# A hybrid decoder layer on one core: the weight products of both half-steps by a block method with seven products

## The chip, the cores and the metric

The kernel runs on one core of one Trainium2 chip. The metric is the device time of that core in microseconds, from launch to end, as the median of several executions. A core has five engines, each with a queue that it works off in order: TensorE (PE, with its weight loads listed as PEld), VectorE (DVE), ScalarE (ACT), GpSimd (POOL) and SyncE (SP), which here only issues DMA transfers. TensorE writes its products to PSUM, which has eight banks of 128 partitions x 512 float32.

## What is computed

512 tokens with 1024 features pass through three parts: a SwiGLU half-step, a mixer (retention heads beside block-sparse attention heads) and a second SwiGLU half-step. All of it is float32. The half-step, with a hidden width of 2816:

```python
def _swiglu(h, w_gate, w_up, w_down):
    return (jax.nn.silu(h @ w_gate) * (h @ w_up)) @ w_down
x = x + 0.5 * _swiglu(_rms(x, ffn1_norm_w[l]), ffn1_w_gate[l], ffn1_w_up[l], ffn1_w_down[l])
```

## The kernel before

Activations lie with their features on the partitions and the 512 tokens along the free axis. Every float32 operand of a product is split exactly into two float32r parts, a high part (a copy on ScalarE, rounded) and a low part (the difference, on VectorE). A product of two such operands is then three matmuls, high x high, high x low and low x high (`mm3`, line 357). Each matmul takes a weight block of 128 x 128 as its stationary operand and all 512 tokens as its moving one.

`ffn` (line 413) is a half-step. For each of 22 blocks of the hidden features it loads the gate and the up weights as chunks of 128 x 1024 (`split_w`, line 329: one DMA of 512 KB on SyncE's queue, one ScalarE copy, one VectorE subtraction) and issues 2 x 8 x 3 = 48 matmuls into two PSUM banks. VectorE and ScalarE then scale by the norm, apply SiLU and multiply, and the result is split into its two parts. For each of 8 blocks of the output features it then loads three chunks of the down weights and issues 22 x 3 = 66 matmuls; VectorE adds half of the sum to the residual, and the next stage's weighted parts are made (`Stream.add`). The last block of the second half-step is done by halves of the tokens, 132 matmuls of 256 columns. The first half-step has 22 x 48 + 8 x 66 = 1584 matmuls, the second 66 more.

The matmuls are started with the unscaled input: the norm's factor per token (`st.r`) is applied behind the products, so that the statistics of the tokens (`Stream.stats`) run beside the first of them.

Nothing is issued in program order. `Plan` (line 63) records every instruction with what it reads and writes, and `_order` (line 193) then runs a list schedule: each engine is modelled with a cost per instruction (`_cost`, line 118), the instruction that was noted first goes first unless the table `DELAYS` shifts its part of the mixer, and an instruction is held back while its tile has no free slot. The instructions are issued in that order, which fixes the order on each engine; on the chip, semaphores make each wait for what it needs. Because `issue` calls all of them from one place, the profile lists them all under line 181.

On-chip memory is 80 tiles of 128 x 512 float32 and three buffers each of 128 x 1024 for a raw weight chunk and its two parts. PSUM has fixed tags: two banks "p", two "s", three "t", one "o".

GpSimd has little to do: sums of squares for the norms and part of the rotations in the mixer. In the body of a half-step it is idle.

## Time and profile before

| | |
|---|---|
| median of 3 runs | 1011.9 us (1011.61 to 1012.08) |
| span of the profiled execution | 1010.4 us, 11674 instructions |
| median less that span | 1.5 us |
| PE busy | 993.1 us (98%), 4524 matmuls |
| DVE busy | 526.2 us (52%) |
| ACT busy | 413.3 us (41%) |
| POOL busy | 88.8 us (9%) |
| granted TensorE clock | 0.998 of full speed |
| DMA | 105.17 MB, mean 104 GB/s |

The span is the time from the first to the last instruction of one profiled execution; the runs' times hold a little more around it. Busy time counts an instruction from its start to its end as the profiler has it. Matmuls are pipelined, so that the busy time of PE and the length of one matmul say little; the distance from one start to the next, or a stretch's length over the matmuls in it, says what one costs. An instruction that is held up by another engine's use of a shared resource is listed as longer, not as waiting.

### The profile page before, as it was taken

Reading aid. Unit: us, or ns where it says so; the run is one execution under the profiler, and the core shown is the slowest. Engines: PE = TensorE matmul, PEld = TensorE weight load, DVE = VectorE, ACT = ScalarE, POOL = GpSimd, SP = SyncE. Lnnn points to the kernel's source line nnn. Section 1 sums busy time; section 2 is a strip of 40 time slices with the busy share of each in tenths; the row PEclk is TensorE's granted clock in tenths of the full one; section 3 lists DMA queues with packets and bytes.
Section 4 is the critical chain, followed back from the end, with each engine's and each line's share of the span. In section 5 each row is a group of like instructions: output and inputs, shape, how many; then the busy total and the mean of one; then the engine's idle time right before and its main releaser. Section 6 shows DMA issues by size and latency. Waiting matters only on the chain.

```text
span 1010.4 us, 11674 instructions
## 1 busy us (share of the span) xinstructions
PE 993.1 (98%) x4524; PEld 812.5 (80%) x4524; DVE 526.2 (52%) x768; ACT 413.3 (41%) x641; POOL 88.8 (9%) x63
## 2 busy tenths in 40 slices
PE   8999999999999999989999999999999999999998
PEld 4888888888888888878887778688888888888888
DVE  7535434534332325587879997855445445432231
ACT  6423223223222225467868876543233233221120
POOL 4000000000010100143213320400000000000000
PEclk9999999999999999999999999999999999999999
DMA  6322322332333463352233211422322322333330
GB/s 222 117 92 84 114 95 84 106 103 78 111 116 105 131 211 115 107 151 66 83 131 115 58 38 53 141 103 86 105 94 94 104 91 97 99 94 110 125 111 26
DMA packets 36407, 105.17 MB, mean 104 GB/s; under 512 B 4480, under 2 KB 6528, under 8 KB 36352
## 3 DMA queue, kind: packets, MB, share of 16 engines
q1 hardware_dynamic: 36352, 104.43, 32.1%
q8 instruction: 35, 0.57, 0.2%
q14 instruction: 20, 0.16, 0.0%
HBM read 97.60 MB, written 4.19 MB: 101 GB/s over the span
## 4 chain that ended last, share of the span: by engine, by line
PE 87%; DVE 7%; ACT 3%; issue 1%; DMA 1%; SPq 0%; DVEq 0%; ACTq 0%
PE ps_p L181 45%; PE ps_s L181 36%; DVE s L181 5%; PE ps_t L181 4%; ACT s L181 2%; PE ps_o L181 2%; DVE wl L181 1%; ACT wh L181 1%; DMA s<-in_x_t_dram 1%; SPq L181 0%; DVE c L181 0%; DVE ad L181 0%; ACT c L181 0%; DVEq L181 0%; ACT cr L181 0%
## 5 line engine op out<-in xcount | busy, mean ns | idle before, releaser
L181 PE MATMUL ps_p<-s,wh 128*128 128x512 f32 (+1 forms) x1548 | 561.8, 392 | 3.1 <-DVE s L181 1.6
L181 PE MATMUL ps_s<-s,wh 128*128 128x512 f32 (+1 forms) x1056 | 399.1, 385 | 0.0
L181 ACT ACTIVATE wh<-raw 128x1024 fp32r<-128x1024 f32 (+4 forms) x186 | 181.0, 976 | 469.7 <-PE ps_p L181 335.7
L181 PEld LDWEIGHTS ps_p<-s,wh 128*128 128x128 f32 x1548 | 289.6, 189 | 67.0 <-DVE s L181 3.4
L181 PE MATMUL ps_p<-s,wl 128*128 128x512 f32 (+1 forms) x774 | 298.3, 392 | 1.7 <-DVE wl L181 1.7
L181 DVE TENSOR_TENSOR wl<-raw,wh 128x1024 fp32r<-128x1024 f32 (+4 forms) x186 | 219.3, 1182 | 131.4 <-ACT wh L181 128.7
L181 PEld LDWEIGHTS ps_s<-s,wh 128*128 128x128 f32 x1056 | 198.6, 188 | 39.5 <-ACT wh L181 0.2
L181 PE MATMUL ps_s<-s,wl 128*128 128x512 f32 (+1 forms) x528 | 203.6, 386 | 1.5 <-DVE wl L181 1.5
L181 PEld LDWEIGHTS ps_p<-s,wl 128*128 128x128 f32 x774 | 145.7, 189 | 32.2 <-DVE wl L181 2.9
L181 ACT ACTIVATE s<-s 128x512 f32<-128x512 f32 (+2 forms) x216 | 134.1, 628 | 77.5 <-DVE s L181 66.8
L181 DVE TENSOR_TENSOR s<-ps_p,s 128x512 f32<-128x512 f32 x72 | 49.5, 688 | 190.8 <-PE ps_p L181 190.0
L181 POOL TENSOR_TENSOR s<-s 128x512 f32<-128x512 f32 x57 | 87.5, 1542 | 376.5 <-ACT s L181 290.6
L181 DVE TENSOR_TENSOR s<-s 128x512 fp32r<-128x512 f32 (+2 forms) x155 | 111.8, 723 | 15.7 <-ACT s L181 8.6
L181 PEld LDWEIGHTS ps_s<-s,wl 128*128 128x128 f32 x528 | 99.1, 188 | 22.7 <-DVE wl L181 3.2
L181 DVE TENSOR_TENSOR s<-ps_s,s 128x512 f32<-128x512 f32 x44 | 30.4, 691 | 52.5 <-PE ps_s L181 50.2
L181 PE MATMUL ps_o<-s 128*128 128x256 f32 (+3 forms) x144 | 39.7, 295 | 2.3 <-DVE s L181 2.1
L181 PE MATMUL ps_t<-wh,s 128*128 128x512 f32 x96 | 33.7, 395 | 0.0
L181 PEld LDWEIGHTS ps_o<-s 128*128 128x128 f32 x144 | 27.3, 189 | 6.8 <-ACT s L181 2.5
L181 DVE SCALAR_TENSOR_TENSOR s<-s 128x512 f32<-128x512 f32 x30 | 24.1, 807 | 11.8 <-ACT s L181 11.5
L181 DVE SCALAR_TENSOR_TENSOR s<-s,cols 128x512 fp32r<-128x512 f32 (+1 forms) x28 | 26.8, 967 | 5.8 <-ACT s L181 5.8
L181 DVE SCALAR_TENSOR_TENSOR s<-ps_p,s 128x512 f32<-128x512 f32 (+1 forms) x9 | 6.0, 662 | 31.1 <-PE ps_p L181 31.1
L181 PE MATMUL ps_s<-s 128*128 128x128 f32 (+3 forms) x64 | 19.0, 336 | 2.8 <-DVE s L181 2.8
(65 smaller groups left out, 387.3 us busy)
## 6 DMA issues: line engine op xcount, KB each, us to landing
raw<-in_wg_dram SPq DMA_DIRECT2D x43, 512.0 KB
raw<-in_wu_dram SPq DMA_DIRECT2D x43, 512.0 KB
raw<-in_wd_dram SPq DMA_DIRECT2D x32, 512.0 KB
raw<-in_w_int_dram SPq DMA_DIRECT2D x20, 512.0 KB
raw<-in_wd_dram SPq DMA_DIRECT2D x16, 384.0 KB
s<-in_rtab_dram SPq DMA_DIRECT2D x16, 256.0 KB
raw<-in_w_inn_dram SPq DMA_DIRECT2D x8, 512.0 KB
raw<-in_w_o_dram SPq DMA_DIRECT2D x8, 384.0 KB
```

What stands on the lines that cost most here:

```text
L181: self.ops.append([eng, cost, lambda: fn(*args, **kwargs), deps, tiles, i + self.delay + DELAYS.get(self.part, 0), self.part])
```

## The change

In 18 of the 22 hidden blocks, and in all of the down products, four block products in two by two (two weight blocks, two halves of the inner dimension, two halves of the 512 tokens) are replaced by the seven-product scheme of Strassen in Winograd's form. `strassen` takes four quarters of a weight matrix, for two matrices at once (`m`: gate and up, or two output blocks), forms four sums and differences of them on GpSimd (eight instructions of 128 x 512 a call), and makes seven products of 2 x 4 x 3 = 24 matmuls with 256 moving columns. Each of the seven weight operands, raw quarters and sums alike, is split into its two parts right before its product. `token_blocks` makes the seven operands on the token side: one half-block as it is, then halves and differences of halves (four GpSimd instructions of 128 x 256 for each pair of inner blocks), each split into its two parts on ScalarE and VectorE. The products are added up partly in PSUM (banks "a", "b", "c") and partly on VectorE.

In the hidden part, nine calls of `hidden` work on the blocks q and q + 9 for q = 4 to 12; the first four blocks (EVEN) run as before. The normalised input is now needed in front of the products, so the moving operands are made from x, the norm weight and `st.r`. The output part runs over the inner dimension in three sections of 8, 8 and 6 hidden blocks (nk = 4, 4, 3), each with two calls for four output blocks each, and adds each section's share to the residual, which is loaded again from DRAM (`was`; for the second half-step it is written to `later` first). The hidden activations are kept in one piece and split when a section starts.

`weave` notes the calls so that the start of the next lies between the later products of the one before. `nc.after` makes an instruction depend, in the schedule alone, on a marked matmul. Weights come in chunks of 128 x 512 with 12 slots for raw ones, 8 for sums, 6 for each part, and 32 slots for token blocks; all share a pool of 98 tiles. The cost model's figures for a matmul and for GpSimd are changed, and the mixer's weights are split by chunks of 512 as well. `DELAYS` is as it was.

```diff
+EVEN = 4
+HALF = (22 - EVEN) // 2
...
                 return max(4 * 107.0, n * 1.675)
-            return max(107.0, n * 0.4167) + 3
+            return max(107.0, n * 0.4167 + 13.3)
...
-        return 45 + n * 2.31
+        return 45 + n * 2.8
...
+        if self.after is not None:
+            deps.add(self.after)
...
-    NS, NRAW, NSPLIT = 80, 3, 3
+    NS = 98
...
-    BANKS = {"p": 2, "s": 2, "t": 3, "o": 1}
-    def slot(dt=F32, shape=(128, 512), stream=None):
-        return nc.tile(sp, list(shape), dt, "s", NS, stream)
+    SLOTS = {"raw": 12, "sum": 8, "wh": 6, "wl": 6, "keep": 4, "row": 8, "block": 32}
+    BANKS = {"p": 2, "s": 2, "t": 3, "o": 1, "a": 2, "b": 2, "c": 2}
+    def slot(dt=F32, shape=(128, 512), use=None):
+        return nc.tile(sp, list(shape), dt, "s", NS, use and (use, SLOTS[use]))
 
     def bank(tag):
-        return nc.tile(pp, [128, 512], F32, "ps_" + tag, BANKS[tag])
+        return nc.tile(pp, [128, 512], F32, "ps", 8, ("ps_" + tag, BANKS[tag]))
...
+        each = 512 // shape[2]
+        raws, hs, ls = [], [], []
+        for a in range(0, shape[1], each):
+            n = min(each, shape[1] - a)
+            tiles = slot(use="raw"), slot(F32R, use="wh"), slot(F32R, use="wl")
+            raw, h, lo = (t[:, :n * shape[2]].rearrange("p (a b) -> p a b", a=n) for t in tiles)
+            for x, to in zip((raw, h, lo), (raws, hs, ls)):
+                to.append(x)
+            if pieces is None:
+                nc.sync.dma_start(raw, src[:, a:a + n])
+                nc.scalar.activation(h, raw, AF.Copy)
+                nc.vector.tensor_sub(lo, raw, f32(h))
...
+    def token_blocks(pairs, gates=None):
+        res = [[] for _ in range(7)]
+        gate = lambda q: setattr(nc, "after", gates and gates[min(q, len(gates) - 1)])
+        for q, (one, two) in enumerate(pairs):
+            gate(q)
+            if q % 2 == 0:
+                bh, bl = slot(F32R, use="block"), slot(F32R, use="block")
+            o = slice(256 * (q % 2), 256 * (q % 2) + 256)
+            nc.scalar.activation(bh[:, o], one[:, :256], AF.Copy)
+            nc.vector.tensor_sub(bl[:, o], one[:, :256], f32(bh[:, o]))
+            res[0].append((bh[:, o], bl[:, o]))
+        def two_blocks(n, t):
+            h, lo = split(t, use="block")
+            for i in range(2):
+                res[n + i].append((h[:, 256 * i:256 * i + 256], lo[:, 256 * i:256 * i + 256]))
+        for q, (one, two) in enumerate(pairs):
+            gate(q)
+            two_blocks(1, two)
+        later = []
+        for q, (one, two) in enumerate(pairs):
+            gate(q)
+            t = slot(use="block")
+            nc.gpsimd.tensor_sub(t[:, :256], one[:, 256:], one[:, :256])
+            nc.gpsimd.tensor_sub(t[:, 256:], two[:, 256:], t[:, :256])
+            two_blocks(3, t)
+            u = slot(use="block")
+            nc.gpsimd.tensor_sub(u[:, :256], two[:, 256:], one[:, 256:])
+            nc.gpsimd.tensor_sub(u[:, 256:], two[:, :256], t[:, 256:])
+            later.append(u)
+        for q, u in enumerate(later):
+            gate(q)
+            two_blocks(5, u)
+        nc.after = None
+        return res
+    def strassen(load, nk, moving, taken):
+        n = nk * 128
+        r = {}
+        for i, j in ((1, 1), (1, 2), (2, 1), (2, 2)):
+            r[i, j] = [slot(use="raw")[:, :n] for _ in range(2)]
+            for m in range(2):
+                load(r[i, j][m], m, i, j)
+        s = [[slot(use="sum")[:, :n] for _ in range(2)] for _ in range(4)]
+        for m in range(2):
+            nc.gpsimd.tensor_add(s[0][m], r[2, 1][m], r[2, 2][m])
+        for m in range(2):
+            nc.gpsimd.tensor_sub(s[1][m], s[0][m], r[1, 1][m])
+        for m in range(2):
+            nc.gpsimd.tensor_sub(s[2][m], r[1, 1][m], r[2, 1][m])
+        for m in range(2):
+            nc.gpsimd.tensor_sub(s[3][m], r[1, 2][m], s[1][m])
+        banks, marks = {}, []
+        def product(tag, w, block, said):
+            start = tag not in banks
+            if start:
+                banks[tag] = bank(tag)
+            p = banks[tag]
+            marks.append(len(nc.ops) + 2)
+            for m in range(2):
+                h, lo = slot(F32R, use="wh")[:, :n], slot(F32R, use="wl")[:, :n]
+                nc.scalar.activation(h, w[m], AF.Copy)
+                nc.vector.tensor_sub(lo, w[m], f32(h))
+                out = p[:, 256 * m:256 * m + 256]
+                for k in range(nk):
+                    o = slice(k * 128, k * 128 + 128)
+                    xh, xl = moving[block][k]
+                    for a, (ww, xx) in enumerate(((h, xh), (h, xl), (lo, xh))):
+                        nc.tensor.matmul(out, ww[:, o], xx, start=start and m + k + a == 0,
+                                         stop=k == nk - 1 and a == 2, skip_group_check=True)
+            taken(said, p)
...
+        yield marks
+        product("a", r[1, 1], 0, "P1")
+        yield marks
+        product("c", r[1, 2], 1, "P2")
+        yield marks
+        product("b", s[0], 3, "P5")
+        product("a", s[1], 4, "U2")
+        yield marks
+        product("a", s[2], 5, "U3")
+        yield marks
+        product("a", r[2, 2], 6, "C21")
+        product("b", s[3], 2, "B")
+        yield marks
+    def weave(calls):
+        run, marks = None, None
+        for call in [*calls, None]:
+            nxt = call and call(marks)
+            if nxt:
+                new = next(nxt)
+            for n in range(2):
+                if run:
+                    next(run)
+                if nxt:
+                    next(nxt)
+            if run:
+                next(run)
+            if nxt:
+                marks = new
...
+        for fb in range(EVEN):
             pieces = [] if first and fb == 0 else None
...
+            hs[fb] = g
...
+        pairs = []
+        for q in range(4):
+            two = []
+            for kb in (q, q + 4):
+                t = slot(use="block")
+                nc.vector.scalar_tensor_tensor(t, x[kb], st.nw[:, kb:kb + 1], st.r,
+                                               op0=OP.mult, op1=OP.mult)
+                two.append(t)
+            pairs.append(two)
+        blocks = token_blocks(pairs)
+        def hidden(one, two):
+            def load(t, m, i, j):
+                nc.sync.dma_start(t.rearrange("p (a b) -> p a b", a=4),
+                                  (wg, wu)[m][(one, two)[i - 1]][:, 4 * j - 4:4 * j])
+            rows = [[slot(use="row") for _ in range(2)] for _ in range(2)]
+            keep = {}
+            def add(i, j, p, old):
+                for m in range(2):
+                    o = slice(256 * m, 256 * m + 256)
+                    nc.vector.tensor_add(rows[i][m][:, 256 * j:256 * j + 256], p[:, o], old[:, o])
+            def taken(what, p):
+                if what in ("P1", "U2", "U3"):
+                    keep[what] = slot(use="keep")
+                    nc.scalar.activation(keep[what], p, AF.Copy)
+                elif what == "P5":
+                    keep[what] = p
+                if what == "P2":
+                    add(0, 0, p, keep["P1"])
+                elif what == "U3":
+                    add(1, 1, keep["P5"], keep["U3"])
+                    g, u = (t[:, 256:] for t in rows[1])
+                    nc.scalar.activation(g, g, AF.Silu)
+                    hs[two] = slot()
+                    nc.vector.tensor_mul(hs[two][:, 256:], g, u)
+                elif what == "C21":
+                    g = rows[1][0][:, :256]
+                    nc.scalar.activation(g, p[:, :256], AF.Silu)
+                    nc.vector.tensor_mul(hs[two][:, :256], p[:, 256:], g)
+                elif what == "B":
+                    add(0, 1, p, keep["U2"])
+                    g, u = rows[0]
+                    nc.scalar.activation(g, g, AF.Silu)
+                    hs[one] = slot()
+                    nc.vector.tensor_mul(hs[one], g, u)
...
+            return strassen(load, 4, blocks, taken)
+        marks = weave([lambda _, q=q: hidden(q, q + HALF) for q in range(EVEN, EVEN + HALF)])
+        nc.after = marks[-1]
...
+            x[db] = slot()
+            nc.sync.dma_start(x[db], was[db])
...
+        def output(f, nk, q, before):
+            ones = (2 * q, 2 * q + 1)
+            final = f + 2 * nk == FB
+            def load(t, m, i, j):
+                nc.sync.dma_start(t.rearrange("p (a b) -> p a b", a=nk),
+                                  wd[ones[m] + 4 * (i - 1), :, f + (j - 1) * nk:f + j * nk, :])
+            def taken(what, p):
+                i, j = {"P1": (0, 0), "P2": (0, 0), "U2": (0, 1), "B": (0, 1), "U3": (1, 1),
+                        "P5": (1, 1), "C21": (1, 0)}[what]
+                o = slice(256 * j, 256 * j + 256)
+                for m, db in enumerate(ones):
+                    y = x[db + 4 * i]
+                    nc.vector.scalar_tensor_tensor(y[:, o], p[:, 256 * m:256 * m + 256], 0.5,
+                                                   y[:, o], op0=OP.mult, op1=OP.add)
+                    if final and last and what in ("P2", "B", "U3", "C21"):
+                        nxt(db + 4 * i, y, o.start, o.stop)
+                if final and not last and what == "B":
+                    for i in range(2):
+                        for db in ones:
+                            nxt(db + 4 * i, x[db + 4 * i], 0, 512)
+            if q == 0:
+                blocks[f] = token_blocks([(hs[f + k], hs[f + nk + k]) for k in range(nk)],
+                                         (before[0],) if f else (marks[4], marks[6]))
+            return strassen(load, nk, blocks[f], taken)
+        f = 0
+        for nk in (4, 4, 3):
+            calls += [lambda before, f=f, nk=nk, q=q: output(f, nk, q, before) for q in range(2)]
+            f += 2 * nk
+        return weave(calls)[-1]
...
+    mark = ffn(s1, x, wg1, wu1, wd1, lambda db, y, a, b: s2.square(y), x_t, load_x)
+    for kb in range(KB):
+        nc.after = mark if kb > 1 else None
+        s2.part(kb, x[kb])
+    nc.after = None
+    saved, later = (dp.tile([KB, 128, S], F32, name=n) for n in ("saved", "later"))
...
+        nc.sync.dma_start(later[db], x[db])
+        later, last=True)
```

## Rows read from the trace of the kernel before

**Rows 1.** The page: span, busy time by engine, chain that ended last.
```profile
span 1010.4 us, 11674 instructions
...
PE 993.1 (98%) x4524; PEld 812.5 (80%) x4524; DVE 526.2 (52%) x768; ACT 413.3 (41%) x641; POOL 88.8 (9%) x63
...
PE 87%; DVE 7%; ACT 3%; issue 1%; DMA 1%; SPq 0%; DVEq 0%; ACTq 0%
```

**Rows 2.** Stretches: start:end length, busy time and count by engine, clock, DMA share, GB/s.
```profile
24.00:70.00 46.00, 45.72 (x201) 37.84 (x202) 25.75 (x33) 17.72 (x22) 0.00 (x0) 1.00 0.33 110
70.00:260.00 190.00, 190.00 (x840) 157.35 (x839) 87.37 (x105) 59.78 (x70) 1.05 (x2) 1.00 0.29 96
260.00:365.00 105.00, 105.00 (x465) 86.97 (x464) 31.80 (x34) 28.55 (x34) 8.10 (x6) 1.00 0.41 128
...
385.00:640.00 255.00, 246.36 (x1201) 198.43 (x1200) 202.03 (x393) 176.99 (x352) 59.30 (x39) 0.99 0.28 91
...
690.00:880.00 190.00, 190.00 (x840) 157.36 (x839) 88.16 (x106) 59.23 (x70) 0.00 (x0) 1.00 0.29 97
```

**Rows 3.** The chain in order of time: start us, length us, what, count.
```profile
315.65 10.65 PE ps_p L181 x47
...
1003.79 3.61 PE ps_p L181 x30
```

**Rows 4.** Instruction groups, shapes apart: shapes xcount | busy us, mean ns | idle before.
```profile
L181 POOL TENSOR_TENSOR s<-s 128x512 f32<-128x512 f32 x57 | 87.5, 1542 | 376.5 <-ACT s L181 290.6 <-DMA s<-s 74.5 <-DVE s L181 9.2
L181 ACT ACTIVATE s<-s 128x512 f32<-128x512 f32 x121 | 75.8, 627 | 22.1 <-DVE s L181 16.9 <-DMA s<-in_x_t_dram 1.3
L181 DVE TENSOR_TENSOR s<-s 128x512 fp32r<-128x512 f32 x87 | 62.3, 718 | 8.1 <-ACT s L181 7.9
...
L181 ACT ACTIVATE s<-ps_p 128x512 f32<-128x512 f32 x8 | 4.7, 590 | 0.0
```

**Rows 5.** Timeline 15.5 to 23.3, DVE and POOL: start us, length us, engine.
```profile
15.62 4.15 DVE L181 SCALAR_TENSOR_TENSOR s<-s,cols 128x512 fp32r<-128x512 f32 x3
...
16.05 7.09 POOL L181 TENSOR_TENSOR s<-s 128x512 f32<-128x512 f32 x4 [1.50 <-ACT s L181]
...
19.70 4.53 DVE L181 TENSOR_TENSOR wl<-raw,wh 128x1024 fp32r<-128x1024 f32 x2
```

**Rows 6.** Timeline 17.9 to 19.8: two instructions of each engine in that stretch.
```profile
16.29 3.49 DVE L181 SCALAR_TENSOR_TENSOR s<-s,cols 128x512 fp32r<-128x512 f32 x2
...
17.60 3.32 POOL L181 TENSOR_TENSOR s<-s 128x512 f32<-128x512 f32 x2
```

**Rows 7.** Timeline 19.5 to 23.3, DVE alone.
```profile
17.99 1.78 DVE L181 SCALAR_TENSOR_TENSOR s<-s,cols 128x512 fp32r<-128x512 f32 x1
```

**Rows 8.** Timeline 576.7 to 583, DVE and POOL in the mixer.
```profile
576.77 1.56 POOL L181 TENSOR_TENSOR s<-s 128x512 f32<-128x512 f32 x1 [2.76 <-ACT s L181]
...
577.09 1.79 DVE L181 SCALAR_TENSOR_TENSOR s<-s 128x512 f32<-128x512 f32 x1
...
579.34 1.28 POOL L181 TENSOR_TENSOR s<-s 128x512 f32<-128x512 f32 x1 [1.01 <-ACT s L181]
579.40 1.77 DVE L181 SCALAR_TENSOR_TENSOR s<-s,cols 128x512 f32<-128x512 f32 x1
...
581.10 0.68 DVE L181 TENSOR_TENSOR s<-ps_p,s 128x512 f32<-128x512 f32 x1
...
581.70 0.67 DVE L181 SCALAR_TENSOR_TENSOR s<-s,ps_s 128x512 f32<-128x512 f32 x1
...
581.92 1.30 POOL L181 TENSOR_TENSOR s<-s 128x512 f32<-128x512 f32 x1 [1.30 <-DVE s L181]
...
582.29 1.47 DVE L181 TENSOR_TENSOR s<-s 128x512 fp32r<-128x512 f32 x1
```

**Rows 9.** Timeline 1002.5 to 1010.5, one VectorE reading of a half bank.
```profile
1003.83 0.42 DVE L181 SCALAR_TENSOR_TENSOR s<-ps_s,s 128x256 f32<-128x256 f32 x1 [6.72 <-PE ps_s L181]
```

**Rows 10.** Timeline 62 to 84, SyncE: one issue of a weight load.
```profile
67.39 0.33 SPq L181 DMA_DIRECT2D raw<-in_wg_dram  x1
```

More of the change, by code (lines that the diff above doesn't have):

```diff
@@ L93, in __init__ @@
         self.part = ""
+        self.after = None
         self.table = None
@@ L256, in _order, with _ended @@
             t, i, *x = heapq.heappop(events)
-            if i == -2:
-                for k in self.tiles[x[0]]:
-                    free[k] += 1
-            if i < 0:
-                continue
-            done += 1
-            over[i] = True
+            now = [(i, x)]
+            while events and events[0][0] <= t:
+                _, i, *x = heapq.heappop(events)
+                now.append((i, x))
+            for i, x in now:
+                done += self._ended(i, x, t, free, over, left, events, succ, at, need, ready)
             while first < n and over[first]:
                 first += 1
-            e = ops[i][0]
-            for x in ops[i][4]:
-                left[x] -= 1
-                if not left[x]:
-                    heapq.heappush(events, (t + self.LAT_FREE, -2, x))
-            for j in succ[i]:
-                at[j] = max(at[j], t + self.LAT[e].get(ops[j][0], self.LAT_ANY[e]))
-                need[j] -= 1
-                if not need[j]:
-                    heapq.heappush(ready[ops[j][0]], (ops[j][5], j))
-                    if at[j] > t:
-                        heapq.heappush(events, (at[j], -1))
-        return order, t
+        return order, t
+    def _ended(self, i, x, t, free, over, left, events, succ, at, need, ready):
+        import heapq
+        if i == -2:
+            for k in self.tiles[x[0]]:
+                free[k] += 1
+        if i < 0:
+            return 0
+        ops = self.ops
+        over[i] = True
+        e = ops[i][0]
+        for x in ops[i][4]:
+            left[x] -= 1
+            if not left[x]:
+                heapq.heappush(events, (t + self.LAT_FREE, -2, x))
+        for j in succ[i]:
+            at[j] = max(at[j], t + self.LAT[e].get(ops[j][0], self.LAT_ANY[e]))
+            need[j] -= 1
+            if not need[j]:
+                heapq.heappush(ready[ops[j][0]], (ops[j][5], j))
+                if at[j] > t:
+                    heapq.heappush(events, (at[j], -1))
+        return 1
     def issue(self):
@@ L347, in mm3, with split @@
         nc.tensor.matmul(ps, wl, xh, start=False, stop=stop)
[L349 to L352 removed]
+    def split(src, n=512, h=None, lo=None, use=None):
+        h = slot(F32R, use=use) if h is None else h
+        lo = slot(F32R, use=use) if lo is None else lo
         nc.scalar.activation(h[:, :n], src, AF.Copy)
@@ L390, in add, with part @@
         def add(self, kb, x, delay=0):
+            self.part(kb, x)
+            self.square(x, delay)
+        def part(self, kb, x):
             w = self.nw[:, kb:kb + 1]
@@ L411, in stats @@
             self.v, self.r = v, rsqrt(v)
-    def ffn(st, x, wg, wu, wd, nxt, first=None, last=False):
-        hs = []
-        for fb in range(FB):
+    def token_blocks(pairs, gates=None):
[32 more added lines that the diff above has]
+        return res
@@ new lines, in weave, with ffn @@
+    def weave(calls):
[13 more added lines that the diff above has]
+                marks = new
+            run = nxt
+        return marks
+    def ffn(st, x, wg, wu, wd, nxt, was, first=None, last=False):
+        hs = [None] * FB
+        for fb in range(EVEN):
@@ L439, in ffn @@
             nc.vector.tensor_mul(g, g, u)
-            hs.append(split(g))
-        for db in range(KB):
-            cuts = [(0, 256), (256, 512)] if last and db == KB - 1 else [(0, 512)]
-            ps = [bank("ps"[(db + i) % 2]) for i in range(len(cuts))]
-            chunks = []
-            for f0 in range(0, FB, 8):
-                n = min(8, FB - f0)
-                wh, wl = split_w(wd[db, :, f0:f0 + n, :], (128, n, 128))
-                chunks += [(wh[:, j], wl[:, j]) for j in range(n)]
-            y = slot()
-            for p, (a, b) in zip(ps, cuts):
-                for fb, (wh, wl) in enumerate(chunks):
-                    hh, hl = hs[fb]
-                    mm3(p[:, a:b], wh, wl, hh[:, a:b], hl[:, a:b], fb == 0, fb == FB - 1)
-                nc.vector.scalar_tensor_tensor(y[:, a:b], p[:, a:b], 0.5, x[db][:, a:b],
-                                               op0=OP.mult, op1=OP.add)
-                nxt(db, y, a, b)
-            x[db] = y
+            hs[fb] = g
```

39 lines of the change are left out of this document (17 added, 22 removed).

## The prediction

> **What bounds the kernel now.** I read the page's head first: TensorE is busy 98% of the span, VectorE 52%, GpSimd 9%, and the chain that ended last lies 87% on TensorE [rows 1]. Busy time of pipelined matmuls proves little, so I went on to the stretches. From 70 to 260 us and from 690 to 880 us, the gate and up products, TensorE never pauses: 840 matmuls in 190.00 us, 226.2 ns each, at full clock. VectorE is busy 46% there, ScalarE 31%, GpSimd not at all, DMA 29% [rows 2]. The down products look the same, and the mixer (385 to 640 us) leaves TensorE only 8.6 us idle. So the two half-steps are TensorE alone, and their time is matmuls times 226.2 ns: 1584 x 0.2262 = 358.3 us for the first, and for the second 1518 x 0.2262 + 132 x 0.1203 = 359.3 us, 717.6 us together.
>
> What the change turns on is the price of a matmul of 256 columns, since it makes nearly all of them that narrow. The chain has a run of each kind: 47 wide ones in 10.65 us, and 30 narrow ones, each with a fresh weight load, in 3.61 us, 120.3 ns each [rows 3]. Two narrow ones cost 240.6 ns against 226.2 for the wide one they replace: 6% of the work is given back to a fixed cost per matmul.
>
> The Trainium skill (TensorE: Matmul & The Clock Gate, Back-to-back issue gap) gives N/2.4 + 2.5 ns for a single matmul, that is 215.8 and 109.2 ns here. The rows disagree, with 226.2 and 120.3. By the page's figures TensorE would save 69 us over both half-steps instead of the 44.6 below; the rows decide.
>
> **TensorE's part.** A half-step keeps 4 x 48 = 192 wide matmuls (43.4 us). The nine hidden calls have 7 x 24 = 168 narrow ones each: 20.2 us a call, 181.9 us in all, where 18 blocks took 195.4. The output part has four calls of 168 and two of 126: 924 x 0.1203 = 111.2 us, where 528 wide ones took 119.4. Sum 336.5 us; both half-steps 673.0 instead of 717.6. If nothing else changed, the span would be 1010.4 - 44.6 = 965.8 us.
>
> **What it adds on VectorE and GpSimd.** GpSimd gets eight additions of 128x512 a call, where it was idle. Alone one takes 1.28 us (at 579.34) [rows 8]; the mean of 57 is 1.54, and VectorE's 512-wide subtraction shows 0.72 in the mean [rows 4] where alone it shows 0.68 and follows the last by 0.60 to 0.61 [rows 8]. VectorE's weight splits grow from what would be eight of 512 columns for such a pair of blocks to 14.
>
> The two engines do not run side by side here. A VectorE instruction with both inputs in SBUF that meets a GpSimd addition waits until that ends: at 577.09 it took 1.79 us, at 579.40 1.77, at 582.29 1.47, instead of 0.68; those with an input in PSUM (581.10, 581.70) kept 0.68 and 0.67, though the last one's second part lies under the addition of 581.92 [rows 8]. GpSimd waits in the same way: four additions from 16.05 take 7.09 us, 1.77 each [rows 5]. In that stretch the engines alternate: VectorE starts at 16.29, 17.99 and 19.70 [rows 5 to 7], 1.70 us for one instruction of each. With VectorE chunks of 1024 the cycle is half of the 4.53 us that two last from 19.70, less 0.04 of overlap: 2.23, so 512 columns more cost 0.53. I take VectorE's hold as 0.54 us per 512 columns and GpSimd's as the 1.17 that is left of 1.70, with fewer columns in proportion, an estimate from the same rows.
>
> The Trainium skill (SBUF — State Buffer, Who interferes with whom) says the same and more: the second to start blocks for the whole of the other's instruction. With the lengths as listed, 1.28 and 0.68, a pair would take 1.96 us; the trace has 1.70, as the start of one overlaps the end of the other. By the page's reading the output part would need some 24 us more per half-step than by mine.
>
> Now the shared time of each stage:
> - A hidden call: 8 x 1.17 on GpSimd, 14 x 0.54 for weight splits and 0.81 for two multiplications, 17.7 us against TensorE's 20.2. It fits at 88%. At worst VectorE stands still for every addition: 14 x 0.61 + 0.95 + seven readings of half banks at 0.34 (0.42 as listed [rows 9], less the 0.08 of overlap) + 9.4 = 21.2 us. Nine calls: 181.9 to 191.
> - A section of the output part with nk = 4: two calls at 9.36 + 7.56 = 33.8 us, and its token blocks: 16 half additions (9.4) and 12 + 4 half splits (7.6). Sum 50.8 us, while TensorE needs 40.4. With nk = 3 by the same way 38.1 against 30.3. Three sections: 139.7 us against 111.2. With all VectorE work outside the additions (28 readings at 0.34 in a section too) it is 63.4, 63.4 and 50.5, together 177.3.
>
> So in the output part the shared access is the limit, 26% over TensorE. Where between the ends? In the contended stretch of rows 5, VectorE worked from 15.62 to about 25.3 (three 512s and three 1024s with four additions): the holds add up to 9.5 of 9.7 us. That is near the low end, and I go a fifth of the way: 183.7 and 147.2. Against the latter stands what is made ahead: eight sum slots hold one call's additions (9.4 us), and the marks let the first section's blocks start three products before the hidden part ends (some 6 us); I take off 15, and add 2 for products behind the last split: 134.2.
>
> **Waits added.** TensorE's queue is in order, so a product whose low part is late holds all products behind it, of both interleaved calls; VectorE's readings of PSUM in turn wait behind blocked subtractions, and bank "a" is written again only when it is read. Inside a call the next call's product covers that (2.9 us against a copy of 0.59 [rows 4]); at the two seams of a half-step, where `weave` starts anew, nothing does: two gaps of about 1 us each, some filled. The first hidden call needs eight scaled inputs and its blocks (4.3 + 17 us shared) before the four wide blocks end, some 32 us after the statistics. 3 us per half-step for all that, 0 to 8 as bounds.
>
> **What is hidden.** ScalarE: 14 splits at 0.63 and about 3 us more a hidden call, 12 of 20.2 us. SyncE issues 136 instead of 68 weight loads per half-step, each half as large, at 0.33 us [rows 10]: 45 us of some 360, at the same bytes. The residual goes through DRAM once more, 24 transfers of 256 KB, 6% more bytes at a DMA share of 0.3; it is loaded beside the last hidden product and the first output ones. By rows 2 (128 GB/s at a share of 0.41, so some 310 in full) the eight loads of a half-step take 7 us; that is what each seam would cost without this cover.
>
> **The mixer** keeps its shift table, but its splits are twice as many and half as long (0.06 us more each on VectorE), its costs in the schedule change, and six of eight input parts wait for the last product; TensorE has the first two blocks' work then (24 x 0.226 = 5.4 us). An order that fits less well costs a part of the idle 8.6 us again: 0 to 12, below nothing to -3. I take 3.
>
> **Sum.** Per half-step 43.4 + 183.7 + 134.2 + 3 = 364.3 us, both 728.6 against 717.6: +11.0. With the mixer +14.0, the span is 1024.4; a run's median lies 1.5 above the profiled span, so **1026 us**. TensorE wins 44.6 us and loses 59 to the neighbours.
>
> **Rivals.**
> 1. *The shared work is done ahead* (faster). The hidden calls leave 2.5 us each, 22 in all. If the order packs without loss, the hidden part takes 181.9 and the output part 139.7 - 15 + 2 = 126.7: 352.0 a half-step, 13.6 us won, 998 us; with all 22 us used, 345 and 984. It decides when hidden and output parts together take under 315.4 us. For it: rows 5 pack almost fully. Against: the slots hold one call, and the sections after the first get their blocks only when the one before gives up its slots.
> 2. *TensorE alone counts.* The engines overlap and only the seams remain: 965.8 + 6 + 1.5, about 973. For it: VectorE and GpSimd are each under 90% on their own (28 x 0.61 + 28 x 0.34 + 8.7 = 35.3 and 16 x 1.28 + 16 x 0.64 = 30.7 of 40.4 us in a section). Against: every meeting in rows 5 to 8.
> 3. *VectorE becomes the bound throughout*, standing still for each addition: 43.4 + 191 + (177.3 - 13) + 3 = 401.7, 86 us lost, with the mixer's 3 it is 1101. For it: VectorE's order is fixed by a model without the meeting, so a blocked subtraction stands ahead of a free reading. Against: the packing of rows 5.
>
> **How the numbers follow.** Two runs of this kernel differ by less than 0.05%, and 0.2% (2 us) is what can be told from no change. Forecast 0.50, with a range of its own from 1008 to 1055; rival 1 0.25 (984 to 1008); rival 2 0.10; rival 3 0.15 (1055 to 1101). The range of 8 in 10 leaves out rival 2 and the upper two thirds of rival 3: 984 to 1065. Faster: rivals 1 and 2 = 0.35; the same 0.05, where the first two cases meet; slower 0.60.
>
> **What would show it.** Narrow matmuls 120 ns apart where TensorE runs. GpSimd's mean well above 1.28 us and VectorE's 512-wide subtractions above 0.68, at or over 1.0 in the output part. TensorE near 100% in the hidden calls (20 to 21 us each), but at 80 to 85% in the output part, where its waits end on VectorE's low parts; the output part longer than the 119 us of before. Wrong if TensorE is as busy there as in the hidden part, if the hidden calls take over 22 us, or if the mixer moves by more than 12.

## The result and the profile after

The changed kernel takes 1095.0 us (median of 4 runs, 1093.0 to 1095.7) against 1011.8 (4 runs): a ratio of 1.082, 95% interval 1.080 to 1.083. It was forecast slower at 1026, with a range from 984 to 1065; it lost six times as much as forecast.

First the page. VectorE is busy 88% where it was 52, GpSimd 54 where it was 9, TensorE 90 where it was 98, and the chain that ended last lies 30% on VectorE [rows 1]. The row PEclk (granted clock by fortieths of the span) is no longer full:

```profile
span 1093.3 us, 18204 instructions
...
PE 980.0 (90%) x6546; PEld 898.2 (82%) x6546; DVE 962.6 (88%) x1415; ACT 578.5 (53%) x1139; POOL 585.1 (54%) x423
...
PEclk9969999999898899999999999898999999898889
...
PE 56%; DVE 30%; ACT 6%; issue 5%; DMA 2%; SPq 1%; DVEq 0%; ACTq 0%
```

Where a part begins and ends can be told by counting matmuls, since each part has a known number of them (the 202nd ends the first four wide blocks, 1512 more the hidden calls, 924 more the output part). From these times, in us (a tenth either way is how they were read):

| part | before | forecast | changed | additions left out | GpSimd writes only | all on VectorE |
|---|---|---|---|---|---|---|
| hidden part, first half-step | 195.8 | 183.7 | 203.3 | 183.1 | 183.1 | 195.4 |
| output part, first | 119.7 | 134.2 | 155.0 | 122.0 | 124.6 | 145.8 |
| mixer | 274.2 | +3 | 280.4 | 281.0 | 281.9 | 282.0 |
| four wide blocks, second | 45.4 | as before | 49.8 | 47.0 | 47.0 | 47.1 |
| hidden part, second | 195.8 | 183.7 | 196.6 | 183.0 | 183.1 | 191.0 |
| output part, second | 120.8 | 134.2 | 149.3 | 118.5 | 117.2 | 140.8 |

(The forecast has 3 us for seams in each half-step beside its two parts.) The loss lies in the output parts, 64 us, and in hidden parts that win nothing, although TensorE has 13.5 us less to do in each. The stretches (columns as in [rows 2]) show what bounds which: the steady hidden calls, then the three sections of the output part.

```profile
80.00:250.00 170.00, 169.26 (x1411) 169.06 (x1410) 152.07 (x193) 87.14 (x167) 108.55 (x70) 1.00 0.33 102
257.30:316.80 59.50, 47.90 (x338) 45.56 (x338) 57.42 (x78) 29.44 (x55) 42.73 (x36) 0.89 0.28 86
316.80:369.20 52.40, 42.63 (x338) 42.08 (x337) 51.37 (x74) 25.32 (x46) 39.97 (x33) 0.93 0.27 79
369.20:412.30 43.10, 34.20 (x254) 33.19 (x253) 35.89 (x63) 15.53 (x32) 15.47 (x12) 0.92 0.37 117
```

From 80 to 250 us TensorE makes 1411 matmuls in 170 us, 120.5 ns each, without a pause: the calls run at TensorE's pace, with GpSimd busy 64% beside VectorE at 89%. In the sections VectorE is busy 57.4 of 59.5 and 51.4 of 52.4 us while TensorE pauses and its clock falls. Five-microsecond stretches show the start of the hidden part:

```profile
50.00:55.00 5.00, 4.61 (x22) 3.67 (x20) 5.00 (x6) 2.88 (x6) 5.00 (x6) 1.00 0.16 52
55.00:60.00 5.00, 0.00 (x0) 0.00 (x0) 5.00 (x5) 1.46 (x3) 5.00 (x4) 0.89 0.72 231
...
65.00:70.00 5.00, 0.00 (x0) 0.00 (x0) 5.00 (x4) 0.80 (x2) 5.00 (x4) 0.50 0.00 0
70.00:75.00 5.00, 2.48 (x11) 2.48 (x12) 5.00 (x7) 0.00 (x0) 1.92 (x2) 0.50 0.31 99
75.00:80.00 5.00, 5.00 (x40) 5.00 (x39) 3.73 (x7) 3.03 (x6) 1.49 (x2) 0.90 0.31 114
```

TensorE has nothing between 55 and 72.5 us, VectorE does not stop, and when TensorE goes on its clock is at 0.50 (the lower of its two levels, 1.2 GHz), 11 matmuls in 2.48 us. The timeline of VectorE, of GpSimd and of TensorE's first narrow matmul there (start, length, in brackets the wait; a row that joins several instructions can be cut off by the end of the window asked for):

```profile
29.24 2.98 DVE L192 SCALAR_TENSOR_TENSOR s<-s 128x512 f32<-128x512 f32 x2 [0.42 <-ACT s L192]
...
38.04 0.74 DVE L192 SCALAR_TENSOR_TENSOR s<-s,cols 128x512 f32<-128x512 f32 x1
...
43.52 4.66 DVE L192 SCALAR_TENSOR_TENSOR s<-s,cols 128x512 f32<-128x512 f32 x4
48.11 3.60 DVE L192 TENSOR_TENSOR s<-s 128x256 fp32r<-128x256 f32 x4
...
52.23 10.23 DVE L192 TENSOR_TENSOR s<-s 128x512 fp32r<-128x512 f32 x8
62.38 0.68 DVE L192 TENSOR_TENSOR s<-ps,s 128x512 f32<-128x512 f32 x1
62.98 10.70 DVE L192 TENSOR_TENSOR s<-s 128x512 fp32r<-128x512 f32 x8
73.60 0.68 DVE L192 TENSOR_TENSOR s<-ps,s 128x512 f32<-128x512 f32 x1
```

```profile
40.61 16.30 POOL L192 TENSOR_TENSOR s<-s 128x256 f32<-128x256 f32 x15 [0.63 <-DVE s L192]
...
56.87 15.05 POOL L192 TENSOR_TENSOR s<-s 128x512 f32<-128x512 f32 x9
```

```profile
72.53 7.65 PE L192 MATMUL ps<-s 128*128 128x256 f32 x49 [17.91 <-DVE s L192]
```

The first row is the end of the norm's factor, at 32.22 us; the first scaled input follows at 38.04. Eight instructions from 52.23, splits but for one multiplication, take 10.23 us, 1.28 each, where such an instruction with nothing beside it takes 0.60; GpSimd's half additions take 1.09 each up to 56.9, and its nine weight additions 1.67 each up to 71.9. VectorE works its queue off in order, and the low part that TensorE waits for ends at 72.47, behind a dozen other splits. The same in the groups; rows before had 0.72 us for the subtraction and 1.54 for the addition [rows 4]:

```profile
L192 DVE TENSOR_TENSOR s<-s 128x512 fp32r<-128x512 f32 x591 | 584.4, 1029 | 44.9 <-ACT s L192 41.0 <-issue 3.6
L192 POOL TENSOR_TENSOR s<-s 128x512 f32<-128x512 f32 x265 | 417.6, 1594 | 417.0 <-ACT s L192 157.2 <-DMA s<-s 84.1 <-PE ps L192 75.2
...
L192 POOL TENSOR_TENSOR s<-s 128x256 f32<-128x256 f32 x120 | 125.5, 1072 | 42.3 <-DVE s L192 23.3 <-PE ps L192 18.4
...
L192 DVE SCALAR_TENSOR_TENSOR s<-ps,s 128x256 f32<-128x256 f32 x168 | 62.5, 414 | 20.0 <-PE ps L192 20.0
```

The chain in order of time passes through these places:

```profile
38.70 16.50 DVE s L192 x18
...
60.71 11.77 DVE s L192 x8
72.53 174.24 PE ps L192 x1438
...
314.56 21.66 DVE s L192 x23
...
994.79 17.08 DVE s L192 x19
```

### The profile page after: what moved, and what is told of

It is laid out like the page before. It is cut to its first block, busy times and chain, and to the rows that moved or that the text cites. A ratio compares the mean times of both kernels' runs of the same rounds, so it can differ in the third digit from the quotient of the medians.

```text
span 1093.3 us, 18204 instructions
## 1 busy us (share of the span) xinstructions
PE 980.0 (90%) x6546; PEld 898.2 (82%) x6546; DVE 962.6 (88%) x1415; ACT 578.5 (53%) x1139; POOL 585.1 (54%) x423
## 4 chain that ended last, share of the span: by engine, by line
PE 56%; DVE 30%; ACT 6%; issue 5%; DMA 2%; SPq 1%; DVEq 0%; ACTq 0%
PE ps L192 56%; DVE s L192 30%; ACT s L192 5%; SPq L192 1%; DMA s<-in_wd_dram 1%; DVE c L192 0%; DMA s<-in_x_t_dram 0%; DMA s<-saved 0%; DMA s<-in_wu_dram 0%; DMA s<-in_w_int_dram 0%; DVE ad L192 0%; ACT L192 0%; ACT L198 0%; DVEq L192 0%; ACT cr L192 0%
## 5 line engine op out<-in xcount | busy, mean ns | idle before, releaser
L192 PE MATMUL ps<-s 128*128 128x256 f32 (+2 forms) x6376 | 965.4, 312 | 99.8 <-DVE s L192 94.4
L192 PEld LDWEIGHTS ps<-s 128*128 128x128 f32 x6376 | 878.9, 197 | 169.2 <-DVE s L192 107.7
L192 POOL TENSOR_TENSOR s<-s 128x512 f32<-128x512 f32 (+2 forms) x417 | 584.1, 1423 | 474.7 <-ACT s L192 157.2
L192 DVE TENSOR_TENSOR s<-s 128x512 fp32r<-128x512 f32 (+5 forms) x767 | 712.4, 976 | 47.8 <-ACT s L192 43.4
L192 ACT ACTIVATE s<-s 128x512 fp32r<-128x512 f32 (+3 forms) x828 | 447.1, 596 | 293.6 <-DVE s L192 245.7
L192 ACT ACTIVATE s<-ps 128x512 f32<-128x512 f32 (+6 forms) x156 | 80.2, 521 | 157.0 <-PE ps L192 145.0
L192 DVE TENSOR_TENSOR s<-ps,s 128x256 f32<-128x256 f32 (+5 forms) x222 | 102.8, 487 | 25.8 <-PE ps L192 16.7
L192 DVE SCALAR_TENSOR_TENSOR s<-ps,s 128x256 f32<-128x256 f32 x168 | 62.5, 414 | 20.0 <-PE ps L192 20.0
L192 DVE SCALAR_TENSOR_TENSOR s<-s,cols 128x512 fp32r<-128x512 f32 (+1 forms) x44 | 47.4, 1105 | 6.2 <-ACT s L192 6.2
L192 ACT ACTIVATE s<-s,c 128x384 f32<-128x384 f32 (+3 forms) x32 | 20.7, 647 | 4.5 <-DVE c L192 4.1
```

The costliest lines, as they stand in the source:

```text
L192: self.ops.append([eng, cost, lambda: fn(*args, **kwargs), deps, tiles, i + self.delay + DELAYS.get(self.part, 0), self.part])
```

## The experiments

The last two kernels below have four executions each; each of the others has one, beside one of the kernel before on the same chip (1010.3 to 1012.0 us). The four executions of the changed kernel lie within 2.6 us, so that a difference of two or three between single ones says nothing.

**Is it the additions on GpSimd, and is it that they read?** Two kernels, the first without the additions, the second with GpSimd writing zeros instead.

```diff
-            nc.gpsimd.tensor_sub(t[:, :256], one[:, 256:], one[:, :256])
...
-            two_blocks(3, t)
+            two_blocks(3, one)
...
+        s = [r[2, 1], r[2, 2], r[1, 1], r[1, 2]]
```

> All GpSimd additions of the block method are left out, on the weight side and on the token side; the products take raw quarters and halves in their place, so the result is not the layer's. Splits, matmuls, transfers and PSUM readings stay in number. Shared access (VectorE instructions with two inputs in SBUF and GpSimd additions exclude each other): the gaps at the starts of the hidden part and of the output sections go, the output part falls from 149 to 155 us to 112 to 120, and the whole to 970 to 995 us with the clock at 0.99. If slots, PSUM banks or TensorE's own seams make the gaps, it stays above 1050. Order alone (a schedule made without the exclusion) expects the same as shared access here; the next three tell them apart.

```diff
-            nc.gpsimd.tensor_add(s[0][m], r[2, 1][m], r[2, 2][m])
...
+        for sm in s:
+            for m in range(2):
+                for _ in range(3):
+                    nc.gpsimd.memset(sm[m], 0.0)
```

> Each GpSimd addition is replaced by three GpSimd writes of zeros to the same tile, some 0.5 us each for 512 columns, so GpSimd stays busy as long as before (about 1.5 us for each addition) but reads nothing from SBUF; the result is not the layer's. Shared access: VectorE's 512-wide subtractions fall back to 0.68 to 0.75 us, the output part to under 125 us, the whole to 970 to 1010 us. GpSimd's length in the chain of dependencies as the cause: the whole stays at 1060 to 1095 us, because the operands come as late as now.

995.3 us without the additions, just over the end of its range, and 999.0 us with writes, inside it. In the second, GpSimd is nearly as busy as before (526 us against 585), in groups of three, and VectorE's subtraction is back at 0.71:

```profile
L192 DVE TENSOR_TENSOR s<-s 128x512 fp32r<-128x512 f32 x591 | 397.4, 713 | 95.4 <-ACT s L192 93.4
...
L192 POOL MEMSET s<- 128x512 f32 x626 | 312.3, 526 | 188.4 <-PE ps L192 92.8 <-DVE s L192 48.6 <-ACT s L192 33.0
```

A section then keeps TensorE nearly busy (the second one, 42.1 us for TensorE's 40.4):

```profile
281.30:323.40 42.10, 40.74 (x338) 40.36 (x338) 35.04 (x72) 25.32 (x46) 33.59 (x98) 1.00 0.31 95
```

So 96 of the 1095 us go when the reading goes, with GpSimd nearly as busy; VectorE's busy time in this section falls from 51.4 to 35.0 us. The writes wait for no weights and no activations, so that what the additions' own latency costs is not shown apart; the 3.6 us between the two runs are little more than the spread. With the additions gone the mixer still takes 7 us more than before, so they are not what makes it longer.

**Which additions?**

```diff
-            nc.gpsimd.tensor_sub(t[:, 256:], two[:, 256:], t[:, :256])
...
+            two_blocks(3, one)
```

> Only the token-side GpSimd additions are left out (the products take the halves themselves; the result is not the layer's), the weight-side ones stay. Shared access: a section with nk = 4 needs 33.8 + 7.6 = 41.4 us of it against TensorE's 40.4, so the output part comes to 115 to 125 us, and the seam before the hidden part loses two thirds of its gap of 18 us: 990 to 1015 us. If the weight-side additions are the trouble, it stays above 1050.

1051.8 us, in the range named for the weight side: without the token side, a fifth of the added columns on GpSimd, the kernel is 43 us faster, and the weight side keeps the larger half. The output parts stayed at 144.1 and 138.1, where 115 to 125 was expected: the estimate of a section without token additions, 41.4 us, was too low, as the one with them was.

**The order of issue.** Two ways: the schedule's model learns the shared access, and the token blocks get later due times.

```diff
-                        if at[i] <= t:
+                        if at[i] <= t and not (i in self.shared and held > t):
...
+                            held = t + self.shared[pick]
```

> The same program, but the list schedule knows that a VectorE instruction with two inputs in SBUF and a GpSimd addition cannot run together (each holds the access for 1.055 and 2.285 ns per column); only the order of issue changes. Order as the cause: the product's weight splits no longer stand behind all the token blocks, the gaps at the starts shrink to a few us, and the whole falls to 1015 to 1040 us. Shared access as a limit of throughput: the sections of the output part still need 51 us of it, only the gap before the hidden part shrinks; 1060 to 1085 us.

1092.5 us, above both ranges. Knowing of the shared access changes little: the one wait of 17.9 us before the hidden part becomes three of 16.6 together. Nor is the rest as it was: the output parts take 162.0 and 155.0, 7 and 6 us more, and the mixer 267.4, which is 13 less than in the changed kernel and 7 less than before. So the mixer's time hangs on the order, and the median alone hides that.

```profile
59.09 0.38 PE L196 MATMUL ps<-s 128*128 128x256 f32 x1 [3.90 <-DVE s L196]
65.76 0.58 PE L196 MATMUL ps<-s 128*128 128x256 f32 x1 [6.29 <-DVE s L196]
72.71 2.50 PE L196 MATMUL ps<-s 128*128 128x256 f32 x10 [6.37 <-DVE s L196]
```

```diff
+            nc.delay = late[1]
             two_blocks(1, two)
```

> The changed kernel with its additions on GpSimd, but the token blocks get later due times in the schedule (75, 95 and 140 places after block 0 for blocks 1 and 2, the sums with 3 and 4, and 5 and 6; 30 to 190 at the later sections), so that the weight splits of the first products, and of the section still running, no longer stand behind all of them in VectorE's queue. Order as the cause of the gaps at the starts: the gap of 18 us before the hidden part falls under 6, the sections gain 2 to 5 us each, 1045 to 1065 us. Shared access as a limit of throughput, whatever the order: what is gained at the start is waited for a few products later, 1085 to 1097 us.

1085.4 us. TensorE starts at once, then waits 5.6, 2.4 and 0.9 us a few products later; the hidden parts take 198.3 and 198.1, the sections of the first half-step 57.1, 53.2 and 41.6. What is gained at the start is waited for later, as a limit of throughput says.

**All additions on VectorE.**

```diff
-            nc.gpsimd.tensor_add(s[0][m], r[2, 1][m], r[2, 2][m])
+            nc.vector.tensor_add(s[0][m], r[2, 1][m], r[2, 2][m])
```

> The whole change, but every addition of the block method, on the weight side and on the token side, is done by VectorE instead of GpSimd. VectorE gets a third more to do (an nk = 4 section 35.3 + 16 x 0.61 + 16 x 0.34 = 50.5 us, over TensorE's 40.4), but no one takes the access from it. Shared access, where a GpSimd addition holds 1.17 us and a VectorE one 0.54: hidden parts at 183 to 187 us, output parts at 130 to 142, the whole 1020 to 1045 us. If the amount of element-wise work is the cause and not the meeting of the two engines, it gets no faster than 1080.

1062.7 us, between the two ranges: VectorE has 360 instructions more and the kernel is 32 us faster. By the forecast's estimate a VectorE addition holds the access for half as long as a GpSimd one (0.54 against 1.17 us), which fits. The rest of the 96 us is then VectorE's own time: its second section lasts 52.0 us, 49.1 of them busy, where 50.5 had been worked out.

```profile
303.80:355.80 52.00, 44.27 (x338) 43.56 (x337) 49.12 (x105) 23.35 (x43) 1.04 (x2) 0.93 0.25 74
```

With the later due times as well:

> The whole change with all additions on VectorE (1062.7 us), with the later due times. Order: hidden parts and sections gain as in the run with GpSimd, 1025 to 1045 us. Throughput: the output sections are VectorE's own 50 us whatever the order, and only the start of the hidden part gains: 1050 to 1063.

1050.7 us, at the foot of the second range, the sections of the first half-step at 53.1, 54.0 and 37.0: of the 12 us that the order gains, 10 come from the hidden parts (190.9 and 185.3).

**Time before the first block.**

```diff
-EVEN = 4
+EVEN = 8
```

> The changed kernel with eight wide blocks in front instead of four and seven hidden calls instead of nine: TensorE has 3 us more to do per half-step, but 43 us more pass before the first token block is needed. If the gap at the start of the hidden part is work that does not fit into the time of three wide blocks, it goes: 18 and 11 us won, 6 paid, 1068 to 1078 us. If the gap is a fixed latency at every change of part, 1097 to 1103.

1063.7 us, 31 less, better than expected. The seven calls take 143.3 us for TensorE's 141.5, in both half-steps, with the additions on GpSimd:

```profile
97.60:240.90 143.30, 141.79 (x1178) 141.33 (x1177) 129.18 (x162) 74.39 (x144) 91.18 (x62) 1.00 0.35 111
240.90:298.70 57.80, 48.16 (x339) 46.08 (x338) 56.98 (x78) 29.47 (x55) 45.23 (x36) 0.88 0.28 89
```

The gap was work that did not fit; the first section, in the second line, is nearly as long as ever.

**The slow clock.** Idle matmuls of zeros, issued ahead of the hidden calls:

```diff
+        fill = bank("o")
+        for i in range(80):
+            nc.tensor.matmul(fill, idle[:, :128], idle, start=True, stop=True)
```

> The changed kernel with 80 matmuls on a tile of zeros, waiting for nothing, issued on TensorE between the four wide blocks and the hidden calls, so that the engine is busy (18 us) in the gap of 17.9 us. If the slow clock behind a gap costs time on the path, each half-step wins the 1.7 us that the 36 narrow matmuls behind it lose (0.225 instead of 0.120 us at first), 3 to 4 us in all: 1090 to 1092. If what comes behind the gap waits for VectorE anyway, no change: 1094 to 1096.

1094.8 us, but inconclusive: they ended 3.6 us early in the first half-step, and the clock in the next 5 us of work was 0.66, against 0.65 without them. With 92 and 50 of them:

> As the run with 80 idle matmuls, where they ended at 69 us, 3.6 before the hidden calls went on, and the clock had fallen to 0.66 in the 5 us from 72.6 all the same; now 92 of them in the first half-step (some 20.5 us, to about 74.5) and 50 in the second (11 us), so that the hidden calls start at full clock. If the slow clock costs time on the path: the first hidden part starts 1 to 2 us later than the 72.5 us of the changed kernel, runs at 120 ns from its first matmul and ends within 0.5 us of it or before, at 256 to 257.5 us instead of 257.3. If TensorE waits for VectorE anyway, no change of the end beyond the later start: 258 to 259 us. The whole: 1091 to 1096 us in both.

1094.4 us. Stretches behind the gap, first with the clock held, then the changed kernel's:

```profile
72.00:77.00 5.00, 4.15 (x34) 4.16 (x35) 5.00 (x8) 1.16 (x3) 1.36 (x2) 1.00 0.17 58
```

```profile
72.50:77.50 5.00, 4.97 (x29) 4.98 (x30) 5.00 (x9) 0.53 (x2) 0.00 (x0) 0.65 0.40 143
```

The first hidden part ends at 256.1 us instead of 257.3, and the output part at 412.6 instead of 412.3. So the slow clock at the start of the hidden part costs 1.2 us there by these two traces, less than the spread of the whole, and by the end of the output part nothing is left of it. The lower clock inside the output sections (0.89 to 0.93) was not held in any run.

**The hidden part alone.** The down products go back to the way before; the hidden activations are split ahead of them.

```diff
+        parts = [split(h) for h in hs]
...
+                    mm3(p[:, a:b], wh, wl, hh[:, a:b], hl[:, a:b], fb == 0, fb == FB - 1)
```

> The block method in the 18 hidden blocks alone, all its additions on VectorE (14 x 0.61 + 0.95 + 2.4 + 8 x 0.61 = 16.8 us a call against TensorE's 20.2); the down products are done as in the kernel before. Shared access: hidden parts 183 to 186 us instead of 195.8, down products 119 to 122: each half-step wins 7 to 12 us, the whole 988 to 1000 us, faster than both kernels. If seams cost by themselves (statistics before the products, slots), the gain is eaten and it stays at 1005 to 1020.

1029.1 us, a miss: hidden parts 195.4 and 191.0, down products 128.5 and 129.3. VectorE was busy without pause from 29 to 69 us, and TensorE's gap before the first product lasted to 64.5; 21 splits in a row from 250.1 to 262.5 stood at the start of the down products, with pauses of TensorE to 256.8. With the weight side on GpSimd:

> As the hidden-only kernel, but the weight-side additions stay on GpSimd (token-side ones on VectorE). In the steady calls the trace of the changed kernel had TensorE without pauses (1411 matmuls in 169.3 of 170 us), so there nothing changes; at the start of the hidden part ten weight-side additions of 1.17 us meet the token splits. Shared access: a gap of 5 to 12 us and a slow clock behind it at each start, 1000 to 1020 us. If only the token-side additions made that gap, it equals the run with all on VectorE.

1039.5 us, a miss too: worse by the start (hidden parts 200.9 and 194.9) and no better elsewhere. And all on VectorE with later due times:

> The hidden-only kernel with all additions on VectorE (1029.1 us), with the same later due times for the token blocks. Its gap of 9.7 us before the hidden part came after VectorE had been busy without pause from 29 to 70 us. Order: TensorE starts the first products at once and the rest of the blocks is made beside them, hidden parts 184 to 188 us instead of 195 and 191: 1010 to 1020 us. Throughput: 1025 to 1031.

1021.2 us, between the two ranges, hidden parts 190.5 and 185.6: order helps here by 8 us.

**A version that gives both seams their time.** Eight wide blocks, seven hidden calls, down products as before, each hidden activation split just before its use with two output blocks at once.

```diff
+EVEN = 8
...
+                    parts.extend(split(h) for h in hs[f0:f0 + n])
+                    for db in dbs:
+                        for fb in range(f0, f0 + n):
+                            mm3(ps[db][0], *chunks[db][fb], *parts[fb], fb == 0, fb == FB - 1)
```

> What the runs so far point to: eight wide blocks in front, the block method in seven hidden calls alone, all its additions on VectorE, the down products as before, with the first two output blocks worked on together and the hidden activations split just ahead of their use. Seven calls take TensorE 141.5 us instead of 152.0. If the two gaps were shared work that did not fit before the first product, both are gone: 8 to 10 us won in each half-step, 992 to 998 us, faster than both kernels. If a seam costs by itself, 1003 to 1015.

> The same with the weight-side additions on GpSimd. A steady call needs 17.7 us of shared access of 20.2: no difference from all on VectorE but 0 to 3 us at the start of the hidden part, 992 to 1001 us. If the meeting of the two engines costs also where it fits, each call takes 21 us and more: 1004 to 1012.

1000.8 us (ratio to the kernel before 0.989, 95% interval 0.987 to 0.990) and 999.2 us (0.988, 0.986 to 0.990): 1.1 and 1.2% below the kernel before, clear of the spread, the first 3 us beyond its range and the second inside. The second one's hidden part and down products:

```profile
98.00:240.70 142.70, 142.01 (x1178) 141.55 (x1177) 121.76 (x168) 76.46 (x147) 66.88 (x43) 1.00 0.37 112
240.70:359.90 119.20, 119.20 (x531) 98.67 (x530) 53.41 (x82) 41.39 (x78) 8.97 (x8) 1.00 0.42 137
```

142.7 us, where 14 wide blocks take 152.0, and 119.2 as before. The weight-side additions on GpSimd cost nothing that can be told where the access has room: the two runs differ by less than their spread.

## Why the prediction was wrong

**Right.** Narrow matmuls at 120.5 ns (120.3 forecast). The two engines exclude each other as read: 1.68 us for each 512-wide addition beside a 512-wide subtraction (four from 65.2 to 71.9), 1.70 forecast; 1.15 for a half addition beside a split (four from 52.3 to 56.9), where 0.59 + 0.54 = 1.13 was put down. The steady hidden call fits, at TensorE's pace. The output part as the place of the loss, slower than the 119 us of before, with VectorE at the limit. The mixer at +6.2, inside its bounds. Also *"I take off 15"* for what is made ahead of the output part: from 229.5 us to the end of the hidden part GpSimd made eight additions and eleven half additions for the first section, 15.8 us by the forecast's hold, and TensorE lost little by it (36 matmuls in 5 us, twice, where 41.5 fit):

```profile
229.50:257.30 27.80, 24.26 (x19) 1.00 0.44 133
...
245.00:250.00 5.00, 4.26 (x36) 4.06 (x35) 5.00 (x7) 2.57 (x6) 3.96 (x3) 1.00 0.51 157
250.00:255.00 5.00, 4.21 (x36) 4.01 (x35) 5.00 (x7) 2.91 (x6) 4.34 (x5) 1.00 0.55 161
```

(The first row is of GpSimd alone.) Rival 2 (TensorE alone counts) is out. Rival 3's range, 1055 to 1101, holds the time measured, by way of the output part; VectorE is not the bound throughout, since the steady calls run at TensorE's pace.

**Wrong, two terms of the sum.**

1. *"3 us per half-step for all that, 0 to 8 as bounds."* The hidden parts take 21.4 and 14.7 us more than TensorE's 181.9; 17.9 and 10.7 of that is the wait before the first product. The step set token blocks of 4.3 + 17 us against 32 us of wide blocks, and both were off. The norm's factor is there at 32.2 us and the wide blocks end at 54.4, which leaves 22. And the access had more to serve than token blocks: from the factor to 72.5 us, where TensorE goes on, also the splits of the wide blocks and of the first products, and ten weight additions for the first two calls. By the forecast's own holds all that adds up to some 38 of the 40 us that pass. With 43 us more ahead of it (eight wide blocks) the wait is gone. It was priced as a latency at a seam, and it was throughput in a window.
2. *"I go a fifth of the way"* between perfect packing, where VectorE reads PSUM beside GpSimd's additions, and none. By the forecast's holds what the two engines ran in the output parts adds up to 130 and 120 us of shared access, around the 126.7 that the sum had (139.7 - 15 + 2). The parts took 155.0 and 149.3: 24 and 29 us over the shared time, where a fifth was 7.5. Against 126.7 to 164.3, the two ends with the same 15 off and 2 added, they lie three quarters and three fifths of the way. In each part VectorE stands idle for 10 us, 9 of them in wait of products; the other 14 and 19 are PSUM readings, of 28 in all, that found no place beside an addition.

```profile
PE ps L192 <- DVE s L192: 30.2, 15, 8.0
...
DVE s L192 <- PE ps L192: 9.4, 16, 2.3
...
939.15:1088.40 149.25, 124.42 (x927) 121.22 (x925) 138.93 (x207) 60.64 (x117) 92.49 (x74) 0.90 0.21 64
```

(Waits in the first output part: who for whom, us, times, the longest; then the stretch of the second.) The stretch of [rows 5], from which the fifth was read, has no PSUM reading and no wait of VectorE in it, so it could not show this packing. That readings stand behind blocked subtractions in VectorE's queue, rival 3's reason, fits; no run tried it apart.

The two add up to 62 of the 69 us between the forecast span and the measured one; most of the rest lies in the second four wide blocks (4.4 us more than before) and in the mixer. What the engines do to each other was right, and what it adds up to was not. Shown by runs is that the additions' reading makes 96 us (the run with writes), that VectorE's own time for the same additions would make 64 of them (all on VectorE), and that the later due times are worth 10. The split of a part into holds, idle time and readings is worked out from the traces with the forecast's holds, and is an estimate.

## What to carry to other kernels

When a change gives work to two engines that share something, add up the shared time of every window that ends at a "first use", not only of the steady loop: all work that the window holds counts, whoever it is for, and the window opens only when its last input is there. Take work that does not need the shared thing (here VectorE's PSUM readings) as hidden beside it only if a row shows such work hidden. A saving on the bound engine is worth taking only in the stages where the others have room: here seven products instead of eight pay in the hidden part (999 us), and lose in the output part, which has a sum, a split and a reading for every few products.

## What the runs showed beside that

GpSimd writing zeros did not slow VectorE's two-input subtractions (0.713 us with 626 writes of 0.526 us, 0.710 with neither writes nor additions), so it is the reading that meets. The Trainium skill (SBUF — State Buffer, Who interferes with whom) says so too, and this trace agrees. In the run with 80 idle matmuls TensorE worked up to 69.3 us, then waited 3.4 us, and the granted clock of the next 5 us was 0.66; with 92 of them it waited 0.9 us, and the clock stayed at 1.00.
